# Gate and up products of a SwiGLU by Strassen's seven block products, in a float32 diffusion backbone on one core

## The chip, the cores and the metric

The kernel runs on one core of a Trainium2 chip. The metric is the device time of one launch in microseconds, the median of several runs. The core has a matrix engine (TensorE, "PE" in the profile, its weight loads "PEld"), VectorE ("DVE"), ScalarE ("ACT"), GpSimd ("POOL") and a queue that issues transfers (SyncE, "SP"). Each engine takes its instructions in the order in which the program issues them; between engines there are only semaphores. Products land in PSUM, which has eight banks; everything else is in SBUF.

## The reference, cut to what matters

Two layers act on 640 tokens (128 of context, 512 of latents) of width 1024. A layer has three sub-layers: a SwiGLU feed-forward, a token mixer, and a second SwiGLU feed-forward. All is float32.

```python
def swiglu(h, wg, wu, wd):
    return (jax.nn.silu(h @ wg) * (h @ wu)) @ wd

x = x + 0.5 * mod[:, :, 0, 2] * swiglu(modnorm(x, 0), P["ffn1_wg"], P["ffn1_wu"], P["ffn1_wd"])
mix, ctx_out = token_mixer(modnorm(x, 1), P, rope, ctx)
x = x + mod[:, :, 1, 2] * mix
x = x + 0.5 * mod[:, :, 2, 2] * swiglu(modnorm(x, 2), P["ffn2_wg"], P["ffn2_wu"], P["ffn2_wd"])
```

`modnorm` is an RMSNorm followed by a scale and a shift that come, like the output gate `mod[..., 2]`, from a product of the conditioning vector with `w_ada` (1024 x 9216 in each layer). The hidden width is 2816, that is 22 tiles of 128. The mixer has windowed attention, a recurrent branch and a Fourier branch, each gated and merged.

## The kernel before

Activations lie feature-major: 8 row tiles of 128 features by 640 tokens, in two halves of 320 tokens. A float32 product is made in three passes over an exact split into a high and a low part (hi·hi, hi·lo, lo·hi), by `mm3` (L201, L202, L203). The normalised input of a sub-layer is kept as `hh` and `hl`. A weight chunk (128 output columns, 1024 inputs) is loaded into one of the `raw` buffers, rounded by ScalarE (`pump`, L149), and its low part is made by VectorE (L155). The split chunk stays in an arena (`WA0` to `WA7`) until its last product.

A feed-forward sub-layer (`ffn`) takes its 22 hidden tiles in three groups, `THIRDS`, of 7, 7 and 8. For each hidden tile f and each half of the tokens it makes the gate product and the up product, 8 row tiles by 3 passes each, and `evac` reads them out: SiLU from PSUM on ScalarE (L498), the product with the up part on VectorE (L499), the high part on ScalarE (L500), the low part on VectorE (L503). After each group, eight down products go over the group's hidden tiles and are added to the residual `x` (`xadd`, L379).

The modulation is 128 tiles of `w_ada`, each loaded by SP and reduced on VectorE by two passes (L259, `ada_step`); `evac` takes one such tile per half of a hidden tile, ahead of the low part of the hidden tile, and the down products one per column tile. The mixers take none.

At the end of a sub-layer, `tail` lets the first half of the tokens lead, so that its norm and modulation (`hmake`: GpSimd L330, VectorE L340 and L347, ScalarE L338 and L342) run beside the last products of the second half. These last products are read out and squared after `hmake`, and `accsplit` closes the sum of squares. A feed-forward that follows makes tile 0 of the first half by `group`, then tile 1, then sends the second half through `norm1` (a product with ones, `post`, `hmake`) while tile 2 of the first half runs, and only then begins the second half. The program order of each engine is the order in which these Python functions issue.

Of the kernel before, what the change touches and what calls it, by code (L numbers as in the profile page):

```python
# [15 lines left out]
F32 = mybir.dt.float32  # L16
# [7 lines left out]
NK = 8                       # 128-row tiles of D_MODEL  # L24
THIRDS = [(0, 7), (7, 7), (14, 8)]
# [26 lines left out]
PUMPS = (2, 5)              # tiles of the next sub-layer's input after which a weight chunk is taken  # L52
AHEAD = 4                    # row tiles by which the first half of the tokens leads in a sub-layer's last products
FILL = 32                    # other products (three passes each) between the attention's projections and scores
NGATE = 2                    # tiles of the gates that lead in a branch (the first branch's beside the attention)
LRU_AT = {"a": {0: 0, 4: 1}, "f": {2: 2, 5: 3}, "r": {}}   # merged tile at which a recurrent tile begins
WA = [f"WA{i}" for i in range(8)]


def _plan():  # L60
    """The weight chunks in the order in which the tensor engine takes them: (key, columns)."""
    out = []
    for l in range(DEPTH):
        for s in (0, 2):
            if s == 2:
                out += [((l, "q", t), 1024) for t in ("k", 0, "v", 1, 2, 3)]
                out += [((l, "xr", j), 1024) for j in range(4)] + [((l, "yr", j), 1024) for j in range(4)]
                for b in "afr":
# [4 lines left out]
                    for d in range(8):  # L73
                        if d in LRU_AT[b]:
                            out += [((l, "lw", LRU_AT[b][d]), 512)]
# [13 lines left out]
PLAN = _plan()  # L89
# [5 lines left out]
class Core:  # L95
# [32 lines left out]
    def pump(self, n=99, loads=99):  # L128
# [11 lines left out]
        while n > 0 and self.n_split < self.n_dma:  # L140
            key = self.order[self.n_split]
            a = self.place(key)
            if a is None:
                return
# [1374 lines left out]
```

## Time and profile before

| | |
|---|---|
| median of 3 runs | 2998.46 us (2995.99 to 3004.15) |
| span of the profiled execution, first to last instruction | 2991.6 us |
| its own time | not listed; the median of the runs is 6.9 us above its span |
| TensorE busy | 2948.7 us, 20137 products |
| VectorE / ScalarE / GpSimd busy | 1657.6 / 1132.1 / 139.7 us |
| mean granted TensorE clock | 0.993 of 2.4 GHz |

A product's duration in the trace overlaps that of the next one, so the time per product is read from the number of products in a window. A busy share is an average over stages: the stage's own window says what bounds it.

### The profile page before, as it was taken

The page shows a single profiled execution, that of the slowest core. Times are in us where ns is not written, and L with a number is a line of the kernel's source. Part 1 is how long each engine was busy: PE and PEld are TensorE (multiplying, and loading weights), DVE is VectorE, ACT ScalarE, POOL GpSimd, SP SyncE. Part 2 cuts the span into 40 slices and gives each one's busy share as a digit, 9 for nine tenths or more (in the row PEclk, how much of TensorE's full clock was granted, in tenths as well). Part 3 has the DMA queues.
Part 4 walks back from the last instruction along what each step waited for, and adds up shares of the span by engine and source line. Part 5 has one row for each costly group of instructions (what it writes and reads, how often), then busy time and mean ns, then how long its engine had stood idle before and what let it go on. Part 6 is the DMA issues. An engine that isn't in the chain of part 4 may idle for free. (4 is left out here: it accounts for less than half of the span.)

```text
span 2991.6 us, 48052 instructions
## 1 busy us (share of the span) xinstructions
PE 2948.7 (99%) x20137; PEld 2894.4 (97%) x20137; DVE 1657.6 (55%) x2912; ACT 1132.1 (38%) x1979; POOL 139.7 (5%) x135
## 2 busy tenths in 40 slices
PE   9999999999999999999999999999999999999998
PEld 8999999889999999999999999998899999999998
DVE  7676665754554567676567643366454646333324
ACT  4222123487473342222242222236865634322222
POOL 5000000200000000000010000021000001000000
PEclk9999999999999999999999999999999999999999
DMA  6454442202223234444314422221121221222221
GB/s 228 144 174 148 154 148 67 95 33 82 76 78 105 73 117 167 136 167 138 109 62 164 146 84 68 75 91 54 54 83 64 82 103 64 79 98 71 79 78 36
DMA packets 90059, 304.53 MB, mean 102 GB/s; under 512 B 10097, under 2 KB 13297, under 8 KB 89841
## 3 DMA queue, kind: packets, MB, share of 16 engines
q1 hardware_dynamic: 87250, 295.89, 29.1%
q10 hardware_dynamic: 2592, 5.57, 0.5%
q8 instruction: 157, 2.57, 0.3%
q14 instruction: 60, 0.49, 0.0%
HBM read 293.29 MB, written 8.13 MB: 101 GB/s over the span
## 5 line engine op out<-in xcount | busy, mean ns | idle before, releaser
L202 PE MATMUL bank<-hl,w 128*128 128x320 f32 x4104 | 1273.7, 310 | 14.5 <-DVE hl L347 14.4
L201 PE MATMUL bank<-hh,w 128*128 128x320 f32 x4104 | 1278.1, 311 | 3.0 <-ACT hh L342 2.4
L203 PE MATMUL bank<-hh,w 128*128 128x320 f32 x4104 | 1272.2, 310 | 0.0
L202 PEld LDWEIGHTS bank<-hl,w 128*128 128x128 f32 x4104 | 774.5, 189 | 21.4 <-DVE hl L347 21.3
L201 PEld LDWEIGHTS bank<-hh,w 128*128 128x128 f32 x4104 | 776.0, 189 | 5.1 <-ACT hh L342 4.0
L203 PEld LDWEIGHTS bank<-hh,w 128*128 128x128 f32 x4104 | 775.1, 189 | 0.3 <-DVE w L155 0.3
L155 DVE TENSOR_TENSOR w<-raw,w 128x1024 fp32r<-128x1024 f32 (+3 forms) x406 | 484.8, 1196 | 490.3 <-ACT w L149 490.0
L149 ACT ACTIVATE w<-raw 128x1024 fp32r<-128x1024 f32 (+3 forms) x406 | 413.5, 1024 | 317.7 <-PE bank L203 293.0
L202 PE MATMUL bank<-hid,w 128*128 128x320 f32 x1408 | 435.0, 309 | 0.0
L203 PE MATMUL bank<-hid,w 128*128 128x320 f32 x1408 | 433.9, 308 | 0.0
L201 PE MATMUL bank<-hid,w 128*128 128x320 f32 x1408 | 433.5, 308 | 0.0
L259 DVE SCALAR_TENSOR_TENSOR junk<-ra,rows 128x1024 bf16<-128x1024 f32 x256 | 312.7, 1221 | 4.4
L500 ACT ACTIVATE hid<-tmp 128x320 fp32r<-128x320 f32 x176 | 83.0, 472 | 585.7 <-DVE tmp L499 585.7
L499 DVE TENSOR_TENSOR tmp<-bank,tmp 128x320 f32<-128x320 f32 x176 | 86.3, 491 | 346.3 <-PE bank L203 332.5
L203 PEld LDWEIGHTS bank<-hid,w 128*128 128x128 f32 x1408 | 264.6, 188 | 0.0
L201 PEld LDWEIGHTS bank<-hid,w 128*128 128x128 f32 x1408 | 264.4, 188 | 0.0
L202 PEld LDWEIGHTS bank<-hid,w 128*128 128x128 f32 x1408 | 264.2, 188 | 0.0
L379 DVE SCALAR_TENSOR_TENSOR x<-bank,mods,x 128x128 f32<-128x128 f32 (+1 forms) x336 | 136.8, 435 | 182.2 <-PE bank L203 182.1
L330 POOL TENSOR_TENSOR tmp<-x,rstd 128x320 f32<-128x320 f32 x96 | 95.4, 1025 | 2289.8 <-DVE rstd L318 2289.8
L498 ACT ACTIVATE tmp<-bank 128x320 f32<-128x320 f32 x176 | 76.7, 436 | 250.8 <-PE bank L203 250.6
L288 ACT ACTIVATE tmp<-x 128x320 f32<-128x320 f32 x80 | 37.7, 472 | 183.0 <-DVE x L379 160.8
L503 DVE TENSOR_TENSOR hid<-tmp,hid 128x320 fp32r<-128x320 f32 x176 | 85.4, 485 | 7.5 <-ACT hid L500 7.5
(258 smaller groups left out, 2786.4 us busy)
## 6 DMA issues: line engine op xcount, KB each, us to landing
raw<-w SPq DMA_DIRECT2D x332, 512.0 KB, 3.6
ra<-ada SPq DMA_DIRECT2D x128, 512.0 KB, 3.8
raw<-w SPq DMA_DIRECT2D x64, 448.0 KB, 3.3
an<-adan SPq DMA_DIRECT2D x10, 512.0 KB, 9.0
spill<-x ACTq DMA_DIRECT2D x16, 320.0 KB, 3.4
x<-spill SPq DMA_DIRECT2D x16, 320.0 KB, 4.2
an<-ada SPq DMA_DIRECT2D x6, 512.0 KB, 10.2
x<-x SPq DMA_DIRECT2D x8, 320.0 KB, 5.0
```

The costliest lines, as they stand in the source:

```text
L149: nc.scalar.activation(t[:, 0, :w], r[:, :w], AF.Copy)
L155: nc.vector.tensor_tensor(t[:, 1, :w], r[:, :w], t[:, 0, :w].bitcast(F32), op=OP.subtract)
L201: mm(out, wh, x[0], start=first, stop=False)
L202: mm(out, wh, x[1], start=False, stop=False)
L203: mm(out, wl, x[0], start=False, stop=last)
L259: self.nc.vector.scalar_tensor_tensor(self.junk, r, 1.0, self.rows[:, c, :], op0=OP.mult, op1=OP.mult, accum_out=self.mods[:, l, ty, c, i ...
L330: nc.gpsimd.tensor_tensor(hx[j], self.x[k][:, sl(half)], self.rstd[half], op=OP.mult)
L379: nc.vector.scalar_tensor_tensor(self.x[d][:, a:b], o[:, a - half * HT:b - half * HT], self.mod(l, i, 2, c, d), self.x[d][:, a:b], op0=OP. ...
L498: nc.scalar.activation(sg, og, AF.Silu)
L499: nc.vector.tensor_tensor(hd, ou, sg, op=OP.mult)
L500: nc.scalar.activation(hid[r][:, 0, s], hd, AF.Copy)
L503: nc.vector.tensor_tensor(hid[r][:, 1, s], hd, hid[r][:, 0, s].bitcast(F32), op=OP.subtract)
```

## The change

Most gate and up products are made for two hidden tiles (f, f+1) at once. The weights of the two tiles form a 2 x 2 block matrix (tile by half of the 1024 inputs), the activations another (half of the inputs by half of the tokens). Strassen's method in Winograd's form makes the four output blocks of a matrix product from seven block products instead of eight. A block product here is four row tiles by three passes, 12 instructions of 320 columns. `classical` leaves the first 6 hidden tiles of the first feed-forward and the first 4 of the three others in the old form; 16 + 18 + 18 + 18 tiles, 35 pairs, are made by `strassen`, for gate and for up.

- Weights: `operand` makes from the two raw chunks of a pair, in six steps, three split chunks of 1024 columns (a, b, c) and one of 512 (e), with four sums of 512 columns in place.
- Activations: `sums` makes once in a feed-forward the three sums T1, T2, T3 (four row tiles of 320 each) and, after the last product in the old form, T4 in the place of a quarter of `hh`. T1 to T3 take `WA4` to `WA7`.
- Outputs: the products of one operand go to four banks, some on top of others; `posts` reads them after each block product and adds them on VectorE; SiLU and the rest then act on 640 columns.
- Order: `slot` is called after each block product (and after each half tile in the old form and each down product). It adds the product's time to a running count, takes off the costs of what it issues (`COST`, in us), and issues the waiting low parts (`bg`, `bg2`), the steps of the operands, the sums and the modulation only while the count allows it.
- Modulation: none beside the pairs. It is taken in the down products of the first two groups, in the old-form tiles of the first feed-forward, and now in the mixers: 12 tiles between the attention's steps and 24 at the gated products. The five `raw` buffers now serve weights and modulation together; the silu'd conditioning rows stay in SBUF instead of being loaded twice.
- Groups: `THIRDS` is now 6, 8 and 8.
- Change of sub-layer: the second half's last products are read out between row tiles of `hmake` (`LAST_AT`), not after it. A feed-forward's second half is normalised by `second_half`, on VectorE and ScalarE without GpSimd, issued right after tile 0; between it and the second half of tile 0 stands tile 1 alone. The down products begin with all but two row tiles of some accumulations (`lead`).

The core of the diff (the old `ffn` lines, `sums`' second part and p3 and p6 of `posts` are left out):

```diff
+LAST_AT = 1
+PUMPS = (4, 6)
...
+MM = 0.147
+PROD = 12 * MM
+COST = {512: 0.65, 640: 0.78, 1024: 1.22, "sums": 1.3}
...
+def classical(l, s):
+
+    return 6 if (l, s) == (0, 0) else 4
...
+        if self.step == 0:
+            if not split("a", r0[:, :1024]):
+                return False
+        elif self.step == 1:
+            if not split("e", r1[:, R], 512):
+                return False
+        elif self.step == 2:
+            if (key, "e") not in self.w:
+                return False
+            tt(r1[:, R], r1[:, L], r1[:, R], op=OP.add)
+            tt(r1[:, L], r0[:, L], r1[:, L], op=OP.subtract)
+        elif self.step == 3:
+            if (key, "a") not in self.w:
+                return False
+            tt(r0[:, L], r1[:, R], r0[:, L], op=OP.subtract)
+            tt(r0[:, R], r0[:, R], r0[:, L], op=OP.subtract)
+        elif self.step == 4:
+            if not split("b", r0[:, :1024], tag=tag0):
+                return False
+        else:
+            if not split("c", r1[:, :1024], tag=tag1):
+                return False
+            del self.raw[key], self.raw[k2]
             self.n_split += 1
...
+    def slot(self, cost, time=PROD, ada=0, early=0):
+
+
+
+        self.paced = True
+        self.nslot += 1
+        self.credit = min(self.credit + time - cost, time)
+        for _ in range(len(self.bg)):
+            if self.credit < self.bg[0][0] / 2:
+                break
+            self.work()
+
...
+        more = True
+        while more:
...
+            if len(self.bg) < 3:
+                n = self.n_done
+                s = self.n_split < len(PLAN) and PLAN[self.n_split][0] == "s" and self.step in (2, 3)
+                if s and self.credit < COST["sums"] / 2:
+                    continue
+                self.pump(1)
+                if self.n_done > n:
...
+        while self.t4 and self.credit > 0.4:
+            if next(self.t4, None) is None:
+                self.t4 = None
+            self.credit -= 1.35
+        while self.bg2 and self.credit > self.bg2[0][0] / 2:
+            self.work2()
+        mod(ada)
...
+    def strassen(self, key, base, post):
+
+        o = [self.bank[base + n][:, :HT] for n in range(4)]
...
+        prods = (("a", 0, b11, 0), ("b", 0, t(2), 1), ("c", 0, t(3), 2), ("c", 1, t(1), 3),
+                 ("a", 1, b21, 0), ("e", 0, t4, 2), ("b", 1, b22, 3))
+        for n, (part, c, x, b) in enumerate(prods):
+            wt = self.get((key, part))
+            if part == "e" and self.t4:
+                for _ in self.t4:
+                    pass
+                self.t4 = None
+            for j in range(4):
+                c0 = c * 512 + j * 128
+                wh, wl = wt[:, 0, c0:c0 + 128], wt[:, 1, c0:c0 + 128]
+                xh, xl = x(j)
+                for i, (w, v) in enumerate(((wh, xh), (wh, xl), (wl, xh))):
+                    self.nc.tensor.matmul(o[b], w, v, start=n < 4 and j + i == 0, stop=j == 3 and i == 2,
+                                          skip_group_check=True)
+            if n in (3, 4, 5, 6):
+                self.done((key, part))
+            post[n](o)
...
+        lead = {}
+        if i != 1:
+            for d in range(3):
+                lead[d, 0] = self.gemm(key(d), n - 2, rhs, 0, stop=False)
...
+        n = len(last)
+        at = {}
+        for j, (d, o) in enumerate(last):
+            at.setdefault(min(6, LAST_AT + 4 - n + j), []).append(lambda d=d, o=o: evac(d, 1, o))
+        self.hmake(nxt[0], nxt[1], 0, range(8), PUMPS, at=at)
...
+    def second_half(self, l, i):
+
+        nc = self.nc
+        self.post((1, self.ones_mm()))
...
+        def mul(k):
+            nc.vector.tensor_tensor(self.xf[k], self.x[k][:, s], self.rstd[1], op=OP.mult)
+            nc.scalar.activation(self.xf[k], self.xf[k], AF.Identity, bias=self.mod(l, i, 0, 1, k),
+                                 scale=self.mod(l, i, 1, 1, k))
+            nc.scalar.activation(self.hh[k][:, s], self.xf[k], AF.Copy)
...
+        def low(k):
+            nc.vector.tensor_tensor(self.hl[k][:, s], self.xf[k], self.hh[k][:, s].bitcast(F32), op=OP.subtract)
...
+
+        def split(dst, src):
+            nc.scalar.activation(dst[0], src, AF.Copy)
+            return lambda: tt(dst[1], src, f(dst[0]), op=OP.subtract)
+
+        lows = []
+        for j in range(4):
+            x12, x22 = self.xf[j], self.xf[j + 4]
+            t1 = self.tmp()
+            tt(t1, x12, f(self.hh[j][:, h0]), op=OP.subtract)
+            tt(t1, t1, f(self.hl[j][:, h0]), op=OP.subtract)
+            new = [split(self.T[1, j], t1)]
+            yield True
+            tt(x12, x22, x12, op=OP.subtract)
+            new.append(split(self.T[3, j], x12))
+            tt(x22, x22, t1, op=OP.subtract)
+            new.append(split(self.T[2, j], x22))
+            yield True
+            for z in lows:
+                z()
+            lows = new
+            yield True
+        for z in lows:
+            z()
+        yield True
+        yield False
+        lows = []
+        for j in range(4):
+            x22 = self.xf[j + 4]
+            tt(x22, f(self.hh[j + 4][:, h0]), x22, op=OP.subtract)
+            tt(x22, x22, f(self.hl[j + 4][:, h0]), op=OP.add)
...
+            def finish(n):
+                tt(up[n], up[n], gate[n], op=OP.mult)
+                h = hidden(f + n)
+                nc.scalar.activation(h[:, 0, :T], up[n], AF.Copy)
+                self.bg2.append((COST[T], lambda: tt(h[:, 1, :T], up[n], h[:, 0, :T].bitcast(F32), op=OP.subtract)))
+
+            def posts(x, isup):
+                U, V = x[0][:, hi], x[1][:, hi]
+
+                def p0(o):
+                    nc.scalar.activation(U, o[0], AF.Copy)
+                    side(0.0)
+
+                def p1(o):
+                    tt(U, U, o[1], op=OP.add)
+                    side(0.47)
+
+                def p2(o):
+                    tt(V, U, o[2], op=OP.add)
+                    side(0.47)
...
+                def p4(o):
+                    nc.scalar.activation(x[0][:, lo], o[0], AF.Copy if isup else AF.Silu)
+                    side(0.0)
+
+                def p5(o):
+                    tt(x[1][:, lo], U, o[2], op=OP.add)
+                    if isup:
+                        finish(1)
+                    else:
+                        nc.scalar.activation(x[1], x[1], AF.Silu)
+                    side(0.47 + COST[T] * isup)
...
+                    os = self.group(keys[:2], 0)
+                    self.pump(1)
+                    evac(0, 0, os[0], os[1], pump=0)
+                    nc.scalar.activation(self.warm, self.one1, AF.Abs_reciprocal_sqrt)
+                    self.second_half(l, i)
+                    unit(1, 0, pump=1)
+                    os = self.group(keys[:2], 1)
+                    self.pump(1)
+                    sums = self.gen = self.sums(False)
+                    evac(0, 1, os[0], os[1], None)
+                    self.slot(1.0, 6 * NK * MM)
+                    unit(1, 1, None)
+                    self.slot(0.5, 6 * NK * MM)
+                    for f in range(2, n):
+                        for half in range(2):
+                            unit(f, half, None)
+                            self.slot(0.5, 6 * NK * MM)
+                if n < nf:
+                    self.flush()
+                    self.t4 = sums
+            for f in range(f0 + n, f0 + nf, 2):
...
+                    self.xadd(l, i, d, half, o)
+                    if d == 5:
+                        self.ada_max = 1
+                    self.slot(0.65 if half == 0 else 0.5, 3 * nf * MM, int(d < 7))
...
+            if u % 4 == 2:
+                self.ada_step(1)
...
@@ -1030,6 +1477,7 @@
                     step()
                     if half == 1 and b == "f":
                         step()
+                self.ada_step(1)
```

## Rows read from the trace of the kernel before

**Rows 1.** Page: busy time, share and instructions of each engine; granted TensorE clock in 40 slices.
```profile
PE 2948.7 (99%) x20137; PEld 2894.4 (97%) x20137; DVE 1657.6 (55%) x2912; ACT 1132.1 (38%) x1979; POOL 139.7 (5%) x135
...
PEclk9999999999999999999999999999999999999999
```

**Rows 2.** Windows of feed-forward stretches: length, engines' busy us (count), clock, DMA share, GB/s.
```profile
1100.00:1500.00 400.00, 400.00 (x2731) 400.00 (x2730) 257.13 (x440) 97.47 (x148) 0.32 (x1) 1.00 0.42 143
...
2600.00:2900.00 300.00, 300.00 (x2049) 300.00 (x2048) 100.42 (x153) 71.39 (x105) 0.00 (x0) 1.00 0.24 80
```

**Rows 3.** Costliest groups by shape on VectorE: busy us, mean ns | idle before.
```profile
L155 DVE TENSOR_TENSOR w<-raw,w 128x1024 fp32r<-128x1024 f32 x332 | 407.2, 1229 | 413.5 <-ACT w L149 413.2
L259 DVE SCALAR_TENSOR_TENSOR junk<-ra,rows 128x1024 bf16<-128x1024 f32 x256 | 312.7, 1221 | 4.4
L499 DVE TENSOR_TENSOR tmp<-bank,tmp 128x320 f32<-128x320 f32 x176 | 86.3, 491 | 346.3 <-PE bank L203 332.5 <-ACT tmp L498 13.8
L503 DVE TENSOR_TENSOR hid<-tmp,hid 128x320 fp32r<-128x320 f32 x176 | 85.4, 485 | 7.5 <-ACT hid L500 7.5
...
L259 DVE DVE_READ_ACCUMULATOR junk<-ra,rows 128x1 f32 x256 | 20.9, 82 | 0.0
...
L1106 DVE TENSOR_TENSOR four<-f,four 128x640 fp32r<-128x640 f32 x8 | 6.6, 825 | 6.9 <-ACT four L1105 6.9
```

**Rows 4.** All groups: the 512-column one on VectorE, and ScalarE's.
```profile
L149 ACT ACTIVATE w<-raw 128x1024 fp32r<-128x1024 f32 (+3 forms) x406 | 413.5, 1024 | 317.7 <-PE bank L203 293.0 <-DMA raw<-w 24.5
...
L498 ACT ACTIVATE tmp<-bank 128x320 f32<-128x320 f32 x176 | 76.7, 436 | 250.8 <-PE bank L203 250.6
...
L954 ACT ACTIVATE rec<-lru 128x640 fp32r<-128x640 f32 x8 | 5.9, 741 | 37.5 <-DVE lru L951 37.5
...
L1081 DVE TENSOR_TENSOR f<-bank,f 128x512 fp32r<-128x512 f32 x8 | 5.5, 683 | 0.0
```

**Rows 5.** Timeline of VectorE: start us, duration us, instruction [idle before].
```profile
1544.45 1.23 DVE L155 TENSOR_TENSOR w<-raw,w 128x1024 fp32r<-128x1024 f32 x1 [0.46 <-ACT w L149]
1545.59 0.48 DVE L499 TENSOR_TENSOR tmp<-bank,tmp 128x320 f32<-128x320 f32 x1
...
1555.81 0.49 DVE L499 TENSOR_TENSOR tmp<-bank,tmp 128x320 f32<-128x320 f32 x1 [3.44 <-PE bank L203]
```

**Rows 6.** Waits of TensorE: us in total, times, longest.
```profile
PE bank L202 <- DVE hl L347: 14.4, 22, 1.1
...
PE bank L201 <- ACT hh L342: 2.4, 3, 1.8
```

**Rows 7.** Windows of 5 us at the change of sub-layer near 1530.
```profile
1525.00:1530.00 5.00, 3.91 (x27) 3.65 (x25) 2.82 (x6) 1.55 (x3) 1.69 (x3) 1.00 0.33 108
1530.00:1535.00 5.00, 3.20 (x10) 2.57 (x11) 5.00 (x7) 1.41 (x3) 5.00 (x6) 0.72 0.00 0
1535.00:1540.00 5.00, 4.78 (x31) 4.51 (x30) 4.64 (x11) 3.08 (x6) 0.77 (x1) 0.94 0.00 0
```

**Rows 8.** Timeline of VectorE at the same change of sub-layer.
```profile
1519.99 0.49 DVE L295 TENSOR_TENSOR tmp<-acc,tmp 128x320 fp32r<-128x320 f32 x1 [0.54 <-ACT tmp L294]
...
1527.65 0.49 DVE L318 SCALAR_TENSOR_TENSOR rstd<-tmp,tmp 128x320 f32<-128x320 f32 x1
...
1531.00 1.14 DVE L347 TENSOR_TENSOR hl<-tmp,hh 128x320 fp32r<-128x320 f32 x1
...
1536.40 0.48 DVE L347 TENSOR_TENSOR hl<-tmp,hh 128x320 fp32r<-128x320 f32 x1
```

**Rows 9.** Windows of a mixer: its attention, then its gated products.
```profile
590.00:700.00 110.00, 110.00 (x813) 94.13 (x812) 60.11 (x158) 89.83 (x222) 0.91 (x1) 1.00 0.16 52
700.00:1020.00 320.00, 318.63 (x2188) 317.68 (x2187) 162.68 (x270) 164.18 (x237) 0.00 (x0) 1.00 0.25 83
```

**Rows 10.** Page: a DMA issue, KB each, median us to landing; a window at the start.
```profile
ra<-ada SPq DMA_DIRECT2D x128, 512.0 KB, 3.8
...
20.00:40.00 20.00, 18.33 (x126) 17.33 (x126) 18.75 (x29) 6.44 (x14) 14.73 (x10) 0.84 0.95 370
```

More of the change, by code (lines that the diff above doesn't have):

```diff
@@ new lines, in steps, with arena_for @@
+    def steps(self, n):
+        while n > 0 and self.n_split < len(PLAN):
+            kind, key, w = PLAN[self.n_split]
+            if not (self.one(key, w) if kind == "c" else self.operand(key)):
+                return
+            self.n_done += 1
+            n -= 1
+    def arena_for(self, key, name):
+        a = self.place(key)
+        if a is None:
+            return None
+        self.free_arenas.remove(a)
+        self.arena[name] = a
+        return self.t(a, [128, 2, 1032], F32R, "w")
@@ new lines, in work2, with flush, operand_blocked, clear @@
+    def work2(self):
+        c, f = self.bg2.popleft()
+        self.credit -= c
+        f()
+    def flush(self):
+        while self.gen and next(self.gen):
+            pass
+        self.gen = None
+    def operand_blocked(self):
+        if self.n_split == len(PLAN) or PLAN[self.n_split][0] == "c":
+            return False
+        key = PLAN[self.n_split][1]
+        return self.step in (2, 3) and (key, "  ea"[self.step]) not in self.w
+    def clear(self):
+        while self.bg:
+            self.work()
+        while self.bg2:
+            self.work2()
@@ L485, in norm1 @@
         self.hmake(l, i, 1, range(8))
+    def second_half(self, l, i):
+        nc = self.nc
+        self.post((1, self.ones_mm()))
+        for ty in (0, 1):
+            self.ada_until(l, i, ty)
+        self.whole()
+        s = slice(HT, 2 * HT)
+        order = [k for j in range(4) for k in (j, j + 4)]
+        def mul(k):
[5 more added lines that the diff above has]
+            nc.vector.tensor_tensor(self.hl[k][:, s], self.xf[k], self.hh[k][:, s].bitcast(F32), op=OP.subtract)
+        for n in range(8 + 2):
+            if n < 8:
+                mul(order[n])
+            if n >= 2:
+                low(order[n - 2])
@@ L490, in ffn, with hidden @@
         hid = {}
-        def evac(f, half, og, ou, fill=0, pump=1):
+        def hidden(f):
             r = f - f0
@@ L510, in unit, with pair, p3, p6 @@
                 self.done((l, i, "u", f))
[L511 to L513 removed]
+            evac(f, half, og, ou, pump)
+        def pair(f):
+            tt = nc.vector.tensor_tensor
+            lo, hi = slice(0, HT), slice(HT, 2 * HT)
+            gate, up = [], []
+            side = self.slot
+            def finish(n):
[14 more added lines that the diff above has]
+                    side(0.47)
+                def p3(o):
+                    tt(V, V, o[3], op=OP.add)
+                    side(0.47)
+                def p4(o):
[5 more added lines that the diff above has]
+                        finish(1)
+                    else:
+                        nc.scalar.activation(x[1], x[1], AF.Silu)
+                    side(0.47 + COST[T] * isup)
+                def p6(o):
+                    tt(U, U, o[3], op=OP.add)
+                    if isup:
+                        finish(0)
+                    else:
+                        nc.scalar.activation(U, U, AF.Silu)
+                    side(0.47 + COST[T] * isup)
+                return p0, p1, p2, p3, p4, p5, p6
+            for n, (a, x) in enumerate((("g", gate), ("u", up))):
+                while n and self.bg2:
+                    self.work2()
+                x += self.tmp2(), self.tmp2()
+                self.strassen((l, i, a, f), 4 * n, posts(x, n))
         self.use_banks(range(8))
```

367 lines of the change are left out of this document (251 added, 116 removed).

## The prediction, on record before the change was run

> **What bounds the kernel now.** I read the page first: TensorE is busy for 2948.7 of 2991.6 us, VectorE for 55% and ScalarE for 38% of the span, and the granted clock is at its upper level in all 40 slices [rows 1]. Since a product's duration overlaps the next, I took its cost from windows inside the feed-forwards: 2731 products in 400 us and 2049 in 300 us, at clock 1.00 with TensorE busy throughout, so 146.5 ns each [rows 2]. In these windows VectorE is busy for 64% (with modulation) or 33% (without): nothing but the number of products sets the pace there. Then I read what TensorE waits for. The longest waits are for the normalised input (14.4 us for `hl`, 2.4 us for `hh`) [rows 6], and they sit where one sub-layer ends and the next begins. Three windows there hold 27, 10 and 31 products where a full window holds 36: 40 products, 5.8 us, part of it at the lower clock level (mean granted clock 0.72 and 0.94 after the idle) [rows 7]. So time is gained where products go away, and lost where VectorE, with more to do, comes late.
>
> **Products removed.** A pair of tiles takes 2 x 96 = 192 products by the old form and 2 x 7 x 12 = 168 by the new. For 35 pairs that is 840 fewer: 840 x 0.1465 = 123.0 us. The products keep their 320 columns and their weight load for each, so I keep the price. That fewer are issued follows from the code; that the time goes with them holds only while nothing else paces the pair, which now lasts 168 x 0.1465 = 24.6 us.
>
> **VectorE in a pair.** One operand: three low parts of 1024 at 1.229 us and, at 0.683 us (the 512-column row), one low part and four sums, 7.10 us; two operands 14.2 us. Reading out: ten operations of 320 columns from PSUM at 0.491 us, 4.9 us. Four operations of 640 columns at 0.825 us, 3.3 us. Together 22.4 us [rows 3, 4], against 8.8 us for the same two tiles before (4 x 1.229 + 4 x (0.491 + 0.485)). That is the high end. The timeline shows the low end: an instruction that waits for nothing starts 1.14 us after the start of a 1.23 us one [rows 5], so some 30 instructions could save 0.09 us each: 19.7 us. Either way it is 80 to 91% of 24.6 us. I count VectorE as the cover that is nearly used up, not as the bound. ScalarE has two operands at 3 x 1.02 + 0.59 us (512 columns taken between the rows of 320 and 640), four reads at 0.44 and four operations at 0.74, 12 us of 24.6: covered [rows 4].
>
> VectorE takes its work in order, so behind each of its ten reads stands the side work, and behind that the next operand, for which TensorE waits. The count lets at most one block product's time (1.76 us) be saved up, and the plan makes an operand part one to two products ahead. An instruction late by 1 us should thus be hidden. For 31 pairs that are not the first of a feed-forward I take 0.2 us each, 6 us; bounds 0 and 1 us each.
>
> **The activation sums.** T1 to T3 are 28 operations at 0.485 us, 13.6 us a feed-forward, spread over some 35 us of old-form products whose own VectorE work is near 19 us: covered, just. T4 is 12 more, 5.8 us, and falls into the first pair, whose sixth block product needs it: 22.4 + 5.8 = 28.2 us where 24.6 are there, 3.6 us too many. By the starts it is 19.7 + 12 x 0.40 = 24.5, nothing too many. I take 2.5 us for each of four feed-forwards, 10 us; bounds 0 and 15 us. [...]
>
> **Change of sub-layer.** Before, the second half's norm was covered by tiles 1 and 2 of the first half; now tile 2 is gone from that place: 48 products, 7.0 us less cover. The chain is otherwise the same: the sum of squares ends at 1520.5, the reciprocal root at 1528.1, the first low part at 1532.1 and the fourth at 1536.9 [rows 8]. While GpSimd runs, VectorE's low parts of 320 columns take 1.14 us, after it 0.48 us [rows 8], so `second_half`, without GpSimd, is quicker: two ScalarE operations a tile at about 0.45 us set a pace of 0.9 us. But it makes tiles in the order 0, 4, 1, 5, 2, 6, 3, 7 and TensorE takes them in the order 0 to 7: tile 3 is ready about 7 x 0.9 + 1 = 7.3 us after the root, instead of 8.7, so the chain gains 1.4 us. 7.0 - 1.4 = 5.6 us worse, at three changes into a feed-forward: 17 us. Reading the last products between the tiles of `hmake` delays tiles 2 to 7 of the first half by up to 6 us, but what TensorE loses there it no longer loses at the sum of squares. Bounds for each: 0 (if the sum of squares comes 5.6 us sooner) and 10 us (all the cover, and 3 us more at the lower clock level).
>
> **Modulation, moved.** A tile costs 2 x (1.221 + 0.082) = 2.6 us of VectorE [rows 3]. In the down products the count admits it only where there is room. In a mixer's gated products, 24 tiles are 63 us beside 163 us of work in 320 us: covered. In the attention, 12 tiles are 31 us; VectorE is busy for 60 and ScalarE for 90 of 110 us there [rows 9], and the next maximum over the scores, the exponential behind it and TensorE's transposes stand behind each. The tiles come every second step, and the steps are pipelined, so I take 2 us a mixer, 4 us; bounds 0 and 31 us a mixer. SP's loads of modulation and weights now share five buffers in the same queue; a load lands in 3.8 us and the queue has moved 370 GB/s where 143 were the most in these windows [rows 2, 10], so nothing for that. The rest (resident conditioning rows, `lead`, groups of 6, 8, 8) adds no product, and TensorE had no wait at the places that it touches: nothing.
>
> **The sum.** -123 + 17 + 10 + 6 + 4 = -86 us on the span of 2991.6, 2905.6. The runs' median stands 6.9 us above that span; on the median of 2998.5 it is 2912 us. A change within 0.3% (9 us) is about what a measurement of this kernel cannot tell from none.
>
> **Rivals.**
> - *Nearly the whole gain.* The added costs stay under 20 us in sum: the read-out between the tiles brings the sum of squares forward, and VectorE has the 19.7 us of its starts. 2876 to 2896 us. For it: the waits of TensorE in the old trace are few and short. Against: tile 2's cover is gone by the program's order.
> - *Modulation in the attention holds the softmax up.* Each tile's 2.6 us passes to TensorE in full: 24 x 2.6 = 62 us instead of 4, 2970 us; half of it, 2939 us. For it: ScalarE is busy for 82% there and stands behind VectorE. Against: TensorE has other products between the steps and no idle time in that window.
> - *VectorE paces the pair (the other side).* Its ten reads each wait for a block product; if side work is not ready to fill that wait, the idle time cannot be made up. In the old form it stood 3.4 us idle before such a read [rows 5], though with nothing else to do. Ten such gaps of 0.56 us bring 22.4 us to 28.0 us, and 35 x 3.4 us is the whole gain of 123 less a little: from there on the change is slower, all the more with the 31 us of the other terms. At 0.7 us a gap the pair takes 29.4 us: 2912 - 6 + 35 x 4.8 = 3074 us. Against: the count always keeps low parts waiting behind the read.
>
> **How the numbers follow.** The forecast (2896 to 2935 us) has 0.52; nearly the whole gain 0.18; the attention, or several terms at their upper bounds short of the old time, 0.17 (2935 to 2990 us); VectorE as the bound 0.13, of which 0.03 falls within 0.3%. Faster is 0.87, the same 0.03, slower 0.10. The range 2880 to 2972 us reaches into the nearly whole gain and over most of the third case and leaves out less than 0.2; the likeliest case's own range is 2896 to 2935 us, predicted 2912.
>
> **What would show it.** Right: some 19,300 products; windows inside the pairs at 146 to 148 ns a product with clock 1.00 and VectorE at 80 to 91%; at the changes of sub-layer, waits for `hl` about 5 us longer each; short waits for weights' low parts in each feed-forward's first pair. Wrong: windows in the pairs with TensorE under 95% busy and waits for VectorE's weights or T tiles throughout (VectorE paces), idle TensorE in the attention, or a change of sub-layer no longer than before.

## The result and the profile after

The changed kernel takes 3013.1 us, the median of 6 runs (3007.8 to 3017.7); the kernel before, on the same chip, 2998.1 us (2996.0 to 3004.2). The ratio is 1.0053, with a 95% interval of 1.0038 to 1.0067: slower by 0.5%, where I had forecast 2912 us. The profiled run took 3017.7 us, its span is 3016.0 us. Below, a ratio is against the kernel before as run beside each kernel; 0.001 is 3.0 us.

The page of the changed kernel, busy time by engine and the granted clock:

```profile
PE 2885.3 (96%) x19297; PEld 2811.9 (93%) x19297; DVE 2137.0 (71%) x3710; ACT 1296.3 (43%) x2206; POOL 116.2 (4%) x111
...
PEclk8999999999999999999999999999999999999999
```

The 840 products are gone (20137 in [rows 1]) and TensorE works 63 us less, yet the span is 24 us longer: 131 us of a span of 3016 without a product, where it was 43. By 840 x 0.1465 us it should work 123 us less; the other 60 us are busy time that has become longer, much of it at the lower clock. The mean granted clock of the profiled runs is 0.977, where it was 0.993. With levels of 2.4 and 1.2 GHz that is some 139 us at the lower one against 42, and half of the difference, up to 48 us, is an estimate of what this cost. So the busy share understates the loss. Windows of the changed kernel: two inside the feed-forwards' pairs, the first mixer's attention, its gated products (busy us and count by engine, clock, DMA share, GB/s):

```profile
1300.00:1500.00 200.00, 200.00 (x1366) 200.00 (x1365) 154.33 (x242) 71.85 (x99) 0.00 (x0) 1.00 0.39 116
2700.00:3000.00 300.00, 300.00 (x2049) 300.00 (x2048) 201.97 (x310) 109.25 (x157) 0.00 (x0) 1.00 0.25 74
590.00:700.00 110.00, 104.06 (x745) 84.70 (x744) 84.86 (x214) 82.78 (x227) 1.08 (x2) 1.00 0.31 92
700.00:1060.00 360.00, 348.23 (x2346) 346.53 (x2345) 234.18 (x397) 177.16 (x254) 0.00 (x0) 0.98 0.38 117
```

Two of these hold the forecast: the pairs run at 146.4 ns a product, to the digit as before [rows 2], with VectorE at 67 to 77%, less than my 80 to 91%. The other two do not: the attention holds 745 products where the same window held 813 [rows 9], and in the gated products TensorE stands idle for 12 us, though VectorE is busy for only 65% there. What TensorE waits for (us in total, times, longest):

```profile
PE bank L409 <- DVE hl L593: 18.3, 24, 1.0
PE bank L455 <- ACT w L250: 16.8, 6, 6.2
PE bank L455 <- DVE w L253: 16.5, 12, 2.9
PE bank L409 <- DVE xh L1356: 16.2, 6, 4.6
PE bank L1253 <- ACT pbuf L1264: 9.2, 19, 1.0
```

Only the first stood in [rows 6] at a similar size, 14.4 us, and its longest wait is 1.0 us: waits for `hl` that are 5 us longer, which I had named as a sign, did not come. New are the weights of the pairs (L455) and the softmax's weights `pbuf`; the recurrent branch's operand `xh` has grown from 1.8 us in 4 waits. How `xh` comes late is to be seen on VectorE's timeline where the attention ends (start, duration, instruction, idle time before it and who ended it):

```profile
700.19 1.23 DVE L498 SCALAR_TENSOR_TENSOR acc<-ra,rows 128x1024 bf16<-128x1024 f32 x1 [1.54 <-DMA ra<-ada]
701.34 0.08 DVE L498 DVE_READ_ACCUMULATOR acc<-ra,rows 128x1 f32 x1
701.46 1.23 DVE L498 SCALAR_TENSOR_TENSOR acc<-ra,rows 128x1024 bf16<-128x1024 f32 x1
...
703.01 1.22 DVE L214 TENSOR_TENSOR w<-raw,w 128x1024 fp32r<-128x1024 f32 x1
704.15 0.82 DVE L1356 TENSOR_TENSOR xh<-xg,xh 128x644 fp32r<-128x644 f32 x1
```

and on TensorE's, with the window behind it:

```profile
705.02 0.63 PE L409 MATMUL bank<-xh,w 128*128 128x322 f32 x1 [4.25 <-DVE xh L1356]
```

```profile
705.00:710.00 5.00, 4.98 (x19) 4.98 (x19) 3.27 (x7) 1.09 (x3) 0.00 (x0) 0.50 0.59 160
```

VectorE first waits 1.54 us for a modulation tile's load, then spends 2.4 us on its two passes; the 0.82 us that TensorE needs stand behind, with 1.5 us of other work between. ScalarE had made the high part of `xh` (L1355) by 696.2. Behind the wait TensorE runs at a granted clock of 0.50 and makes 19 products in 5 us, where a full window holds 36. The Trainium skill ("PSUM — Partial Sum Buffer", Engine vs sequencer instructions) states that VectorE's queue is strictly first in, first out; the trace agrees: VectorE idles up to 700.19, while the weight's low part at 703.01 and `xh` at 704.15 had had their inputs since 695.6 and 696.2.

In the first pair of a feed-forward it is T4 (L829, L830, L803) that stands in front. Windows of the changed kernel there:

```profile
1605.00:1610.00 5.00, 4.03 (x26) 3.59 (x26) 4.14 (x9) 1.37 (x3) 0.00 (x0) 1.00 0.00 0
1610.00:1615.00 5.00, 3.00 (x19) 2.48 (x18) 2.68 (x4) 3.53 (x5) 0.00 (x0) 1.00 0.03 4
1615.00:1620.00 5.00, 3.75 (x15) 3.35 (x14) 2.49 (x3) 0.00 (x0) 0.00 (x0) 0.51 0.45 142
```

and VectorE's timeline in them:

```profile
1606.13 1.11 DVE L803 TENSOR_TENSOR hl<-xf,hh 128x320 fp32r<-128x320 f32 x2
...
1608.30 0.69 DVE L270 TENSOR_TENSOR raw<-raw 128x512 f32<-128x512 f32 x1
...
1610.80 0.69 DVE L276 TENSOR_TENSOR raw<-raw 128x512 f32<-128x512 f32 x1
1612.67 1.23 DVE L253 TENSOR_TENSOR w<-raw,w 128x1024 fp32r<-128x1024 f32 x1 [1.18 <-ACT w L250]
1616.14 0.49 DVE L893 TENSOR_TENSOR tmp<-tmp,bank 128x320 f32<-128x320 f32 x1 [2.25 <-PE bank L455]
```

T4's operations have pushed the sums of the second operand (L270 to L276) back, ScalarE splits after them (1.18 us of waiting), then VectorE, and these three windows hold 60 products instead of 3 x 36 = 108. Nobody is saturated: VectorE is busy for 9.3 of the 15 us and itself waits for TensorE. The granted clock has then fallen to 0.51, its lower level, 1.2 GHz.

In the down products before a pair the same happens with modulation tiles; VectorE's timeline in the third feed-forward:

```profile
1646.55 1.22 DVE L498 SCALAR_TENSOR_TENSOR acc<-ra,rows 128x1024 bf16<-128x1024 f32 x1 [2.03 <-DMA ra<-ada]
...
1674.09 1.22 DVE L498 SCALAR_TENSOR_TENSOR acc<-ra,rows 128x1024 bf16<-128x1024 f32 x1
...
1679.52 0.69 DVE L276 TENSOR_TENSOR raw<-raw 128x512 f32<-128x512 f32 x1
```

ScalarE's next split (L250) starts at 1680.32, after 13.75 us of idle time that this sum (L276) ends, and the first pair begins with TensorE's longest wait, 6.2 us for that high part:

```profile
1681.43 0.90 PE L455 MATMUL bank<-T,w 128*128 128x320 f32 x2 [6.22 <-ACT w L250]
```

The 10 us from 1675 hold 4 products. Loads have a part in this too: the two splits before it started at 1661.27 and 1665.94, when their weights had landed. Last, the change of sub-layer of [rows 7] in the changed kernel:

```profile
1530.00:1535.00 5.00, 2.82 (x16) 2.04 (x15) 3.92 (x11) 3.67 (x8) 0.00 (x0) 1.00 0.01 3
1535.00:1540.00 5.00, 4.33 (x18) 4.07 (x19) 2.50 (x5) 3.33 (x6) 0.00 (x0) 0.66 0.35 105
...
1545.00:1550.00 5.00, 4.58 (x28) 3.83 (x27) 4.11 (x11) 4.73 (x9) 0.00 (x0) 1.00 0.00 0
1550.00:1555.00 5.00, 3.66 (x15) 2.94 (x16) 2.75 (x6) 4.85 (x9) 0.00 (x0) 0.87 0.00 0
1555.00:1560.00 5.00, 5.00 (x29) 5.00 (x29) 1.07 (x3) 2.03 (x4) 0.00 (x0) 0.79 0.02 3
```

Against 36 a window these lack 20 + 18 + 8 + 21 + 7 = 74 products, 10.8 us, where 40 were lacking: 5 us worse, near my 5.6.

### The profile page after: what moved, and what is told of

Its sections match the earlier page's. It is cut to its first block, busy times and chain, and to the rows that moved or that the text cites. A ratio compares the mean times of both kernels' runs of the same rounds, so it can differ in the third digit from the quotient of the medians.

```text
span 3016.0 us, 47195 instructions
## 1 busy us (share of the span) xinstructions
PE 2885.3 (96%) x19297; PEld 2811.9 (93%) x19297; DVE 2137.0 (71%) x3710; ACT 1296.3 (43%) x2206; POOL 116.2 (4%) x111
## 4 chain that ended last, share of the span: by engine, by line
PE 71%; DVE 17%; ACT 6%; issue 3%; DMA 2%; POOL 0%; ACTq 0%; DVEq 0%; SPq 0%; POOLq 0%
PE bank L455 27%; PE bank L409 14%; PE bank L408 14%; PE bank L410 14%; DVE acc L498 3%; DMA ra<-ada 2%; DVE w L214 2%; DVE tmp L586 1%; DVE hl L593 1%; DVE w L253 1%; ACT pbuf L1264 1%; DVE x L627 1%; ACT w L210 1%; DVE att L1258 1%; DVE acc L1706 1%
## 5 line engine op out<-in xcount | busy, mean ns | idle before, releaser
L409 PE MATMUL bank<-hl,w 128*128 128x320 f32 x1864 | 587.8, 315 | 19.5 <-DVE hl L593 18.3
L408 PE MATMUL bank<-hh,w 128*128 128x320 f32 x1864 | 590.5, 317 | 6.7 <-ACT hh L762 4.1
L410 PE MATMUL bank<-hh,w 128*128 128x320 f32 x1864 | 583.0, 313 | 3.2 <-DVE w L214 3.2
L455 PE MATMUL bank<-hh,w 128*128 128x320 f32 x2240 | 506.9, 309 | 0.2 <-ACT hh L802 0.2
L214 DVE TENSOR_TENSOR w<-raw,w 128x1024 fp32r<-128x1024 f32 (+1 forms) x266 | 311.9, 1177 | 208.6 <-ACT w L210 208.4
L250 ACT ACTIVATE w<-raw 128x1024 fp32r<-128x1024 f32 (+1 forms) x280 | 256.8, 944 | 466.7 <-DVE raw L276 357.3
L410 PE MATMUL bank<-hid,w 128*128 128x320 f32 x1408 | 435.0, 309 | 1.9 <-DVE w L214 1.9
L408 PE MATMUL bank<-hid,w 128*128 128x320 f32 x1408 | 435.0, 309 | 0.0
L455 PE MATMUL bank<-T,w 128*128 128x320 f32 x2520 | 396.6, 316 | 33.4 <-ACT w L250 16.8
L455 PEld LDWEIGHTS bank<-T,w 128*128 128x128 f32 x2520 | 383.8, 193 | 38.5 <-DVE w L253 20.1
L409 PEld LDWEIGHTS bank<-hl,w 128*128 128x128 f32 x1864 | 357.8, 192 | 29.3 <-DVE hl L593 26.4
L455 PEld LDWEIGHTS bank<-hh,w 128*128 128x128 f32 x2240 | 378.5, 188 | 0.5 <-ACT hh L802 0.5
L253 DVE TENSOR_TENSOR w<-raw,w 128x1024 fp32r<-128x1024 f32 (+1 forms) x280 | 298.2, 1088 | 110.6 <-ACT w L250 110.6
L408 PEld LDWEIGHTS bank<-hh,w 128*128 128x128 f32 x1864 | 358.1, 192 | 10.2 <-ACT hh L762 6.7
L410 PEld LDWEIGHTS bank<-hh,w 128*128 128x128 f32 x1864 | 357.8, 192 | 3.7 <-DVE w L214 3.7
L210 ACT ACTIVATE w<-raw 128x1024 fp32r<-128x1024 f32 (+1 forms) x266 | 268.1, 1012 | 197.6 <-PE bank L410 140.0
L455 PE MATMUL bank<-hl,w 128*128 128x320 f32 x1120 | 347.2, 310 | 5.7 <-DVE hl L803 5.7
L498 DVE SCALAR_TENSOR_TENSOR acc<-ra,rows 128x1024 bf16<-128x1024 f32 x256 | 313.6, 1225 | 31.6 <-DMA ra<-ada 27.0
L410 PEld LDWEIGHTS bank<-hid,w 128*128 128x128 f32 x1408 | 264.4, 188 | 2.7 <-DVE w L214 2.7
L408 PEld LDWEIGHTS bank<-hid,w 128*128 128x128 f32 x1408 | 264.5, 188 | 0.5 <-DVE tmp L917 0.5
```

The source lines that it names most:

```text
L210: nc.scalar.activation(t[:, 0, :w], r[:, :w], AF.Copy)
L214: nc.vector.tensor_tensor(t[:, 1, :w], r[:, :w], t[:, 0, :w].bitcast(F32), op=OP.subtract)
L250: nc.scalar.activation(t[:, 0, :w], src, AF.Copy)
L253: tt(t[:, 1, :w], src, t[:, 0, :w].bitcast(F32), op=OP.subtract)
L408: mm(out, wh, x[0], start=first, stop=False)
L409: mm(out, wh, x[1], start=False, stop=False)
```

## The experiments

My theory after the traces (A): a modulation tile is 2.6 us on VectorE and a wait for its load, and in its new places it holds back the attention, the recurrent branch and the next operands. Theory B: the seven-product form's own vector work takes the gain. Theory C: weights are late, since they share buffers and queue with modulation.

**Modulation left out: of the mixers, of everything, and of the kernel before.** The tiles' list is emptied without loads or passes; the factors are set to 0.5 once.

```
 def queue_ada(self, l, i, types):
-    for ty in types:
+    for ty in ():
```

(for the mixers alone: the tile is taken off the list where `ada_step(1)` stood in the attention and in `merge`).

> The changed kernel, with the modulation tiles that it makes in the mixers (attention and gated products) left out; the factors that they would make stand at 0.5, all the rest of the work stays. Theory A (a modulation tile is 2.6 us of VectorE, taken in order, plus the wait for its load, and it delays the attention and the recurrent branch): the two mixers' lost TensorE time falls from some 71 us to the 21 us of the kernel before, so about 2963 us. Theory B (the seven-product form itself, its VectorE work in the pairs, sums and first pairs, takes the gain): no more than 10 us of 50 come back, about 3005 us or above. Theory C (five buffers shared with the weights' loads make weights late): between, 2985 to 2995 us, since the loads of modulation go away as well.

Measured: 2952.8 us, ratio 0.9854 [0.9831, 0.9878].

> The changed kernel with all 128 queued modulation tiles left out, in the feed-forwards too; the factors stand at 0.5. Theory A: the mixers' 50 us and, in the down products and the first pairs that follow them, another 20 to 30 us come back: about 2935 to 2945 us. Theory B: 2990 us or above. Theory C cannot be told from A by this run alone.

Measured: 2931.1 us, 0.9777 [0.9758, 0.9796].

> The kernel before with the same 128 modulation tiles left out, as a control of what modulation costs there. Theories A, B and C: within 0.3% of the kernel before (2990 to 2998 us), since its TensorE waits are not at modulation. Lower than 2985 us would mean that the price of modulation is not the new places' alone.

Measured: 3000.3 us, 1.0009 [0.9998, 1.0019]. The same 128 tiles cost nothing in their old places and 83 us (1.0053 less 0.9777) in the new ones; 60 of these in the mixers. A holds; B is left with what remains, 2931 us against 2875 (2998 less 123).

**Two loads ahead in the mixers.**

```
 def mixer(self, l):
+    self.ada_max = 2
```

> The changed kernel, with two modulation loads allowed ahead instead of one while the mixers run; nothing is left out. If the wait for the load is what costs (1 to 3.8 us at a tile), 20 to 25 us come back: about 2990 us. If it is the 2.6 us of each tile that VectorE is occupied, about 5 us: 3008 us. Theory C, weights short of buffers: slower than the changed kernel, over 3015 us, since only three buffers are then left for weights.

Measured: 3003.7 us, 1.0023 [1.0011, 1.0036]. VectorE's waits for these loads fall from 27.0 us (18 times) to 9.0 us (6 times), and 9 us come back, half of the waits taken away. The 9 us are sure to some 6, so they cannot be told from my 5 us for occupation alone, but they are clear of the 20 to 25. C is out as far as it is short buffers: one less for the weights did not make the kernel slower.

**Attention and gated products parted.**

```
             if u % 4 == 2:
-                self.ada_step(1)
+                self.ada_skip()
```

> The changed kernel with only the attention's modulation left out (12 tiles a mixer; their factors stand at 0.5). It parts the 60 us that leaving out both the attention's and the gated products' modulation gave. By the trace of the changed kernel the attention lost some 16 us to it and the recurrent branch some 35: then 2993 to 2999 us. If instead the attention, whose softmax stands behind VectorE, is the main cost (my rival of the prediction): 2975 us or less. If the delays are not additive (the gated products would absorb what the attention no longer loses): above 3003 us.

Measured: 2980.8 us, 0.9933 [0.9916, 0.9951]: 36 us for the attention, 24 for the gated products. The attention's tiles cost more than its own stretch shows. Window of this run:

```profile
590.00:700.00 110.00, 110.00 (x817) 93.06 (x816) 69.36 (x187) 88.14 (x237) 2.11 (x2) 1.00 0.18 58
```

and its wait for `xh`:

```profile
PE bank L409 <- DVE xh L1362: 7.4, 4, 2.6
```

The window gains 72 products, 10.5 us, and of six waits for `xh` the two longest, one after each attention, are gone as well: VectorE carried its delay out of the attention into the recurrent branch. The first of these, 4.25 us, and the 17 products (2.5 us) that the window behind it lacked at the lower clock, make 17 us with the 10.5, of the 18 a mixer.

**The sums.** Both on the kernel without modulation (2931 us): T4 left out; then T1 to T3 too.

```
         yield False
+        return
         lows = []
         for j in range(4):
             x22 = self.xf[j + 4]
...
-        t = lambda n: lambda j: self.T[n, j]
+        t = lambda n: b11
```

> The changed kernel with all queued modulation left out, as in the run that gave 2931 us, and without T4 as well: its 12 VectorE and 4 ScalarE operations in each feed-forward are left out. In that run TensorE loses some 33 us in the four first pairs. If T4 in the first pair is what costs there (28 us of VectorE where 24.6 are there), 20 to 30 us come back: 2901 to 2911 us. Rival: the weights' operands are prepared late because the classical products ahead left VectorE no room; then T4's absence gives back under 10 us: 2921 us or above.

Measured: 2902.5 us, 0.9688 [0.9674, 0.9703].

> As the run without T4, and T1 to T3 left out as well: the products of sums read the first half's rows instead, so 40 VectorE and 16 ScalarE operations less in each feed-forward. My prediction took T1 to T3 for covered: then within 3 us of the run without T4. The rival (T1 to T3 take the room in which the first pair's weights would be prepared): 8 us or more below it. Either way, what then stands above 2875 us (2998 less 123) is the price of the rest: changes of sub-layer, start, steady pairs.

Measured: 2901.8 us, 0.9682 [0.9666, 0.9698]. T4 costs 27 us, T1 to T3 nothing that can be told from 0 (2 us, sure to some 7). That it is T4's place and not VectorE's time is seen in two windows of one first pair, with T4 (the kernel without modulation):

```profile
1548.00:1578.00 30.00, 24.20 (x147) 22.70 (x147) 20.50 (x34) 11.55 (x19) 0.00 (x0) 0.94 0.21 67
```

and without:

```profile
1531.00:1561.00 30.00, 28.22 (x193) 27.95 (x192) 19.74 (x28) 12.39 (x19) 0.00 (x0) 1.00 0.29 93
```

VectorE's busy time differs by 0.8 us, TensorE's products by 46, 6.7 us. The Trainium skill ("Trainium Kernel Development and Optimization", Best Practices) advises against judging TensorE's distance from its limit by the busy share of its matmuls. Here the first window has it busy for 81% with 72% of the 205 products that fit.

**T4 in the down products** (modulation left out).

```
 def classical(l, s):
-    return 6 if (l, s) == (0, 0) else 4
+    return 6
...
+            if n == nf:
+                self.flush()
+                self.t4 = sums
             self.clear()
```

> The changed kernel with all queued modulation left out (2931 us with nothing else changed). The first third's six tiles are all in the old form in every feed-forward (24 products more in three of them, 72 x 0.1465 = 10.5 us), and T4 is made during that third's down products, where VectorE has little else, instead of in the first pair. If T4's place in the first pair is its whole cost (28.6 us by the run without T4), this is that run's 2902 us plus 10.5: about 2913 us. If T4 costs by VectorE's time wherever it stands, no gain: 2930 to 2940 us.

Measured: 2906.9 us, 0.9688 [0.9666, 0.9711]: all of T4's cost is gone, though 72 products more are made. The 10.5 us of the 72 added products show in part only: the run without T4 still had 4.5 us of waits for L253 in its first pairs, this one has none. The same vector work costs 27 us in the first pair and, to within some 9 us, nothing in the down products. Three pairs fewer and a first pair that now comes after the down products are part of this edit; what they did alone was not measured.

**Modulation placed otherwise, first try.** A tile is split in its two passes (`ada_half`, 1.3 us).

```
-            if u % 4 == 2:
-                self.ada_step(1)
+            if u >= 2:
+                self.ada_half()
...
-                self.ada_step(1)
+                    if b == "r":
+                        self.ada_step(1)
+                    elif d in ADA_AT[b]:
+                        self.ada_half()
```

> The changed kernel with nothing left out; only the mixers' modulation is placed otherwise: in the attention half a tile (1.3 us) at each step instead of a tile (2.6 us) at every second one, in the first two branches half tiles only where no recurrent tile begins, in the third branch (which has no recurrent tile beside it) two tiles at each row tile, and two loads ahead instead of one. If it is where the 2.6 us stand in VectorE's order that costs, 35 to 45 of the 56 us that leaving them out gave come back: 2968 to 2980 us. If VectorE's total work in the mixers is what costs, it stays above 3000 us.

Measured: 2993.8 us, 0.9992 [0.9980, 1.0003], 18 us back, half of what I expected. The mixers' losses fell, but two tiles a row tile in the third branch, up to its last, now made the merged output late (3.6 us, `mg`), and nothing was done about the feed-forwards.

**Modulation in the pairs.** The placing of the run above, but with none in the attention; a tile at the end of a pair's gate and of its up part; T4's sums earlier.

```
-                    side(0.47 + COST[T] * isup)
+                    side(0.47 + COST[T] * isup, ada=1)
```

> Nothing left out. The placing of the run before without any modulation in the attention; instead a tile at the end of each block product group of a pair where the running count has room, one a row tile in the down products with the load a step earlier; and T4's two sums a row moved ahead of the first pair, so that only its splits stay in it. If the pairs have the room that the windows show (VectorE 70 to 86% busy there): all of the mixers' 56 us, some 10 of the down products' 21 and 10 of the first pairs' 33: about 2940 us. If a pair with 2.6 us more is paced by VectorE, each of some 30 such pairs loses 1 to 2 us: 2970 to 2990 us.

Measured: 3105.4 us, 1.0366 [1.0351, 1.0382], far worse than either figure. Windows of this run:

```profile
230.00:240.00 10.00, 5.70 (x38) 5.19 (x36) 8.26 (x15) 4.11 (x6) 0.00 (x0) 0.95 0.01 3
240.00:250.00 10.00, 6.37 (x31) 5.97 (x32) 4.44 (x6) 1.39 (x3) 0.00 (x0) 0.71 0.44 157
```

TensorE's largest wait in it (us in total, times, longest):

```profile
PE bank L456 <- DVE w L254: 95.0, 52, 6.9
```

and VectorE's timeline in the two windows:

```profile
238.69 1.22 DVE L501 SCALAR_TENSOR_TENSOR acc<-ra,rows 128x1024 bf16<-128x1024 f32 x1
...
239.95 1.23 DVE L501 SCALAR_TENSOR_TENSOR acc<-ra,rows 128x1024 bf16<-128x1024 f32 x1
...
241.10 1.22 DVE L254 TENSOR_TENSOR w<-raw,w 128x1024 fp32r<-128x1024 f32 x1
245.52 0.49 DVE L902 TENSOR_TENSOR tmp<-tmp,bank 128x320 f32<-128x320 f32 x1 [3.20 <-PE bank L456]
```

The low part (L254) that TensorE needs next stands behind two passes. TensorE waits 6.7 us for it, 2.4 of them for the passes, and does half of its products in these 20 us, though VectorE is busy for 64%. Over the whole kernel its waits for these low parts (L253 in the changed kernel) grow from 16.5 us in 12 waits to 95.0 us in 52. The placing in the down products and T4's sums were changed in the same run, and their shares were not parted. VectorE's free time in the pairs (23 to 33% of the windows above) was real and of no use at that point of the order.

**The rest of the change alone**, all gate and up products in the old form.

```
-            for f in range(f0 + n, f0 + nf, 2):
-                pair(f)
+            for f in range(f0, f0 + nf) if f0 else ():
+                for half in range(2):
+                    unit(f, half, None)
+                    self.slot(0.5, 6 * NK * MM)
```

> The rest of the change alone: nothing left out, but the gate and up products all in the old form (840 more products, no sums, no T tiles), with the running count, the six-tile first third and the modulation where the changed kernel has it. Theory A (modulation's new places cost by themselves, whatever the form of the products): the kernel before's 2998 us, plus some 45 us in the mixers and 8 at the start, 3045 to 3060 us. Theory B (VectorE falls behind only through the seven-product form): 2995 to 3010 us.

Measured: 3095.4 us, 1.0320 [1.0303, 1.0336], more than A had. Its waits:

```profile
PE bank L1253 <- ACT pbuf L1264: 16.8, 23, 1.6
...
PE bank L409 <- DVE xh L1356: 13.7, 6, 3.1
```

So the seven-product form makes the kernel 80 us faster with all the rest in place (1.0320 to 1.0053), and the rest of the change alone costs 96. How much of the 96 is modulation and how much the new order of the old form was not parted.

**All placed.** T4 in the down products; half tiles in the attention, in the Fourier branch's input products and at four row tiles each of the first two branches; the third branch without its last row tile; in the feed-forwards only where the count has room. The edit does two things more: two loads ahead in the mixers, and at the last two block products of an operand the running count is credited 1 us instead of 1.76 (`side(..., 1, room=1.0)`).

```
+ADA_AT = {"a": (1, 2, 6, 7), "f": (0, 3, 6, 7), "r": (0, 1, 2, 3, 4, 5, 6)}
...
-            while n > 0 and self.credit > 0 and self.ada_ready and self.ada_slot[0] + 1 < self.nslot:
-                self.ada_step(1)
-                self.credit -= 2 * COST[1024]
+            while n > 0 and self.credit > room and self.ada_ready and self.ada_slot[0] + lead < self.nslot:
+                self.ada_half()
+                self.credit -= COST[1024]
```

> Nothing left out. T4 in the down products as in the run before; modulation in halves of 1.3 us: at each attention step, at each half of the Fourier branch's four input products, at row tiles where no recurrent tile begins (three half-tile pairs fewer than in the changed kernel's first two branches), a whole tile a half row tile in the third branch but not at its last; in the feed-forwards only where the running count has room, in the old-form tiles too; none in the pairs. With modulation's places as the cause: 2913 us plus some 13 us a mixer and 5 to 15 us in the feed-forwards: about 2950 us, 1.5% below the kernel before. If VectorE's total work is the cause: 2990 us or more.

Measured: 2942.4 us, 0.9809 [0.9787, 0.9831]: 1.9% faster than the kernel before. Its page, and its longest waits:

```profile
PE 2856.8 (97%) x19369; PEld 2790.6 (95%) x19369; DVE 2097.9 (71%) x3656; ACT 1282.8 (44%) x2194; POOL 117.1 (4%) x111
```

```profile
PE bank L410 <- DVE hl L600: 18.9, 21, 1.0
PE bank L411 <- DVE w L215: 9.2, 4, 5.4
PE bank L1223 <- ACT qraw L1100: 8.2, 2, 4.4
PE bank L410 <- DVE xh L1364: 5.9, 6, 2.0
```

VectorE does 2098 us of work where the changed kernel has it do 2137, the same 71%, and the kernel is 73 us faster by the ratios. Three pairs fewer, earlier loads and the stricter count are part of that and were not parted from the placing. But VectorE is as busy as before, so it was not its share of the time that cost. The mean granted clock is back at 0.991.

## Why the prediction was wrong

The gain of the products was forecast rightly, and more than all of it was given back. By the ratios, from the changed kernel down: 1.0053 to 0.9933 (attention's modulation, 36 us), to 0.9854 (gated products', 24), to 0.9777 (the feed-forwards', 23), to 0.9688 (T4, 27), to 0.9682 (T1 to T3, 2). What is left is 95 us below the kernel before, 28 short of 123. Each ratio is sure to about 0.002, 6 us, and a step, the difference of two, to some 7 to 9 us. Each price holds the wait and the slower products at the lower clock behind it, for which the sum had no term outside the bounds of the change of sub-layer.

- *840 x 0.1465 = 123 us*: right. The counts are as forecast, and both windows in the pairs keep the price.
- *VectorE in a pair, 6 us for the steady ones*: too much, if anything; those windows lose nothing. The rival that VectorE paces the pair fell.
- *Gated products: "24 tiles are 63 us beside 163 us of work in 320 us: covered"*: this step failed, 0 against 24 us. I compared sums over a stretch. VectorE had the room in it, but not at the point where a tile was put, in front of a short operation that TensorE needed at once.
- *Attention, 2 us a mixer*: the mechanism was in the text and as a rival, the term was taken at its low end; 18 a mixer were measured, of which the window shown holds 10.5; the rest fell behind the attention, in the wait for `xh` and at the lower clock after it, where I did not look. This rival's half, 2939 us, would have been the better base.
- *Down products: "the count admits it only where there is room"*: failed as well. The count holds durations, but no wait for a load and not the tiles that have to be made at once before the first down product. The run without any modulation gives 23 us for the feed-forwards together; how much of it is the loads and how much the passes was not parted.
- *Shared buffers and queue, nothing*: failed by some 9 us (two loads ahead; sure to 6). I compared GB/s. With one load in flight, issued when the tile before is done, what counts is the 3.8 us to landing [rows 10] against the distance of two tiles. The Trainium skill ("DMA: Bandwidth & Descriptors", Rules for kernel authors) says to issue a load early and wait for it late. The runs agree: with two loads ahead VectorE's waits for them fell by 18 us.
- *Activation sums, 10 us (bounds 0 and 15)*: T1 to T3 covered, as said; T4 27 us, beyond the bound, because the bound was again VectorE's sum (28.2 us against 24.6), not its order, and left out the lower clock after the wait.
- *Change of sub-layer, 17 us*: right in kind, too large in sum. At the one shown it is 5 us. Counted in windows of 15 to 40 us over all three, 223 products are missing where 159 were: 64 x 0.1465 = 9 us.
- *"The rest ... nothing"*: of the 28 us that stay without modulation and sums, 9 are the changes of sub-layer. The start, which the sum put at nothing, is 8: the window from 40 to 100 us of that run holds 358 products where the kernel before held 414, and TensorE waits 5.3 us there for weights of the first old-form tiles (L410 3.2, L408 2.1). Another 4.4 us are waits for weights in the second block product of three first pairs; the remaining 7 or so were not tested.

Of the signs of being right that I had named, the number of products, their price and weights' waits in the first pair came; VectorE's 80 to 91% and the longer waits for `hl` did not. Of the signs of being wrong, idle TensorE in the attention came.

## What to carry to other kernels

Room on an in-order engine is a place in its order, not a share of a window: before moving work, find what will stand behind each moved instruction, who waits for that, and whether its own operand has landed. Price the extra delay at every such place in full first, and let cover be proved there. When a change saves on the bounding engine and moves work on another, run each part alone: here the new form was worth 80 us and its companions cost 96.

## What the runs showed of the hardware that was not expected

- A few short waits brought TensorE's clock down behind them: the two windows from 1605 hold 26 and 19 products, with no wait longer than 1.3 us, and the next 5 us ran at a granted clock of 0.51 (1.2 GHz), 15 products in 3.75 us of busy time, 250 ns each instead of 146. By the mean clocks, this is up to 48 us in the changed kernel, an estimate, a third of the 147 us (123 and 24) that its span stands above the forecast gain.
- A delay of VectorE outlives the stretch that made it: taking modulation out of the attention alone gave back 36 us, of which the window of the first attention shows 10.5, so some 21 for both.
